# Stores on ScalarE's queue, a pinned order of the first feed-forward products, and the input ahead of the first weight tiles, in a two-block transformer kernel

## The chip, the cores and the metric

The kernel runs on one core of a Trainium2 chip. The metric is the device time of one execution in microseconds, as the median of several runs. The engines are TensorE (PE), VectorE (DVE), ScalarE (ACT), GpSimd (POOL) and SyncE (SP). Every engine takes its own instructions in order. A transfer (DMA) is started by an instruction in the queue of an engine; in the kernel before, all transfers are started by SP.

## What is computed

Two blocks on a sequence of 1024 tokens with 1024 features, all in float32. The part around the main change is the feed-forward of the first block and what stands before it:

```
h = h + concat(o, y) @ w_out
u2 = rmsnorm(h, ln2_g)
a, b = split(u2 @ w_gate_upffn, 2)          # 1024 x 5632
h = h + (silu(a) * b) @ w_down
h = h + sigmoid(rmsnorm(h, ln3_g) @ w_ple_gate) * (p @ w_ple_proj)
```

The first block begins with `rmsnorm(x, ln1_g) @ w_in`; the second one (gated spatial mixing, a convolution and window attention) starts from a layer norm of the first block's result.

## The kernel before, in words

**Split products.** Every float32 operand is split into a hi and a lo part (`Weights.split`, lines 119 to 141, and `split`, lines 343 to 352: ACT copies the hi part, DVE subtracts to get the lo part). `mm3` (line 321) does three matmuls per 128 rows of the contraction: hi x hi (L327), the second operand's lo part (L328), the first operand's lo part (L329). A group of four such k steps is 12 matmuls.

**Order.** The text of the kernel gives each instruction a priority, in the order of the program. A planner (`schedule_with_timeline_sim`, line 1698) runs through the program with its own durations and appends to each engine's queue what is ready, by priority. `keep_in_program_order` ties an instruction behind the one traced before it on its engine. On the chip each queue is then followed strictly.

**The start** (`run`, line 1586): the identity, then `load_x(0)`, which loads four blocks of x (512 KB each) and puts the first tile of `w_in` between the second and the third; then `load_constants`, with `ln1_g`; then two more weight tiles. `norm_in` (line 475) transposes x on PE (L487), splits the columns times `ln1_g` (L350, L351) and saves copies of them (`save_xT`, L519); the squares for the norm are L500. `proj` then does the first products.

**Before the feed-forward** (lines 1615 to 1619): the out projection of the second half of the tokens goes on while `first_operands` makes the operands A11 and A12 from the first half. Then `ple_proj` (line 909, 16 products of six matmuls from `pT`, each copied from PSUM by ACT, L923, and stored to `ppT`, L924) is interleaved with `other_operands` (line 868). That one normalizes the second half (L854) and makes S3 (L885), A22, S1 (L889), S2 (L893) and S4 (L897): for each of four column groups one DVE subtraction or addition in place, then a hi copy on ACT and a lo subtraction on DVE (L347, L348).

**The feed-forward** (`ffn_up`, line 962) works on 22 tiles f of 128 hidden columns with seven products of 12 matmuls each in place of eight (the scheme of Strassen and Winograd). The two token halves give A11, A12, A22, S1 to S4; the two weight tiles give B11, B21, B22 and T1 to T4, made in `up_weights` (line 928) with four POOL subtractions (L946, L947, L948, L951) and four splits. The four PSUM banks of a tile are X = A11 B11 + A12 B21, Z = S3 T3 + A22 T4, V = S1 T1 + S4 B22, Y = S2 T2. Tiles with even f use the PSUM group g, which `ple_proj` uses too, and the weight buffers hi0 to hi2 and lo0 to lo2; odd tiles use group x and three slots `wo`.

**Slots.** Operand tiles of 8 KB per partition are taken from a list of slots, first in, first out. At the end of `other_operands` the list holds, in this order, the slots of a21, a11, a12 (the activations of the two halves, overwritten in place on the way to S1, S2 and S4) and of `stat`. f=0 takes a21's slot for B22; f=1 takes a11's for B11 and B21, a12's for T1 and T3, and `stat`'s for T2 and T4. A tile in a slot can be written when the last reader of the former tile is done. For a11 these are the S2 split of its fourth group (L348) and the fourth L897.

**Buffers.** Six buffers of 128 x 512 (`t512`) rotate among all short-lived tiles, the copies of L923 among them; three raw buffers take weight tiles (L95), and a load waits until the former raw tile has been read. All loads and stores are in SP's queue, so a waiting load holds back the stores behind it. `spill_x2` (line 1168) copies the transposed result of the first block and stores it to `xres` (L1182), 16 times.

Of the kernel before, what the change touches and what calls it, by code (L numbers as in the profile page):

```python
# [22 lines left out]
NF = FFN // 128  # L23
# [145 lines left out]
class Kernel:  # L169
# [148 lines left out]
        return cols[-4:] + cols[-8:-4]  # L318


    def mm3(self, ps, pairs, start=True, stop=True, more=False):


        mm = partial(self.nc.tensor.matmul, skip_group_check=True) if more else self.nc.tensor.matmul
        n = len(pairs)
        for i, ((lh, ll), (rh, rl)) in enumerate(pairs):
            mm(out=ps, lhsT=lh, rhs=rh, start=start and i == 0, stop=False)  # L327
            mm(out=ps, lhsT=lh, rhs=rl, start=False, stop=False)  # L328
            mm(out=ps, lhsT=ll, rhs=rh, start=False, stop=stop and i == n - 1)  # L329

# [100 lines left out]
    def load_vectors(self, names):  # L431

        nc, I = self.nc, self.I
        rows = self.t512()
        ps = self.psx()
        c0 = self.vcol[names[0]]
        r = 0
        for name in names:
            a = I[name]
            n = int(np.prod(a.shape)) // 128  # L440
            flat = a if len(a.shape) == 1 else (a[0] if len(a.shape) == 2 else a[0].rearrange("a b -> (a b)"))
            nc.sync.dma_start(out=rows[r:r + n, 0:128], in_=flat.rearrange("(n p) -> n p", p=128))
            r += n
        nc.tensor.transpose(ps[:, 0:r], rows[0:r, 0:128], self.ident[0:r, 0:r])
        nc.vector.tensor_copy(out=self.vec[:, c0:c0 + r], in_=ps[:, 0:r])
# [15 lines left out]
    def load_x(self, hf):  # L461
        xt, xs = [], []
        for j in range(2):
            t = self.slot([128, 2, D], F32, "x", base=True)
            for i in range(2):
                r0 = hf * NH + (2 * j + i) * 128
                self.nc.sync.dma_start(out=t[:, i, :], in_=self.I["x"][0, r0:r0 + 128, :])
                xt.append(t[:, i, :])
                if hf == 0 and len(xt) == 2:
                    self.wts.load()  # L470
            xs.append(t)
        self.x_tiles[hf] = (xt, xs)
        return xt, xs
# [435 lines left out]
    def ple_proj(self, pt):  # L909

        nc, W = self.nc, self.wts
        yield
        for m in range(8):
            if m % 4 == 0:
                w2 = W.get("w_ple_proj", 0, 2, m * 128, 512)
                if m == 0:
                    W.ahead()
            w = [x[:, :, m % 4 * 128:m % 4 * 128 + 128] for x in w2]
            for hf in range(2):
                ps = self.psg()  # L920
                self.gemm(ps, w, self.pT[hf])
                o = self.t512()
                nc.scalar.activation(out=o, in_=ps, func=ACTF.Copy)  # L923
                nc.sync.dma_start(out=self.ppT[hf, :, m, :], in_=o)  # L924
                yield
        self.release(*pt)

# [34 lines left out]
    def ffn_up(self, A):  # L962

        nc = self.nc
        self.up_slots = self.up_last = None

        def product(ps, a, b, more=False):
            (ah, al), (bh, bl) = A[a], B[b]
            self.mm3(ps, [((bh[:, k, :], bl[:, k, :]), (ah[:, k, :], al[:, k, :])) for k in range(4)], not more,
                     more=more)  # L970

        def copy(ps):
            t = self.t512()
            nc.scalar.activation(out=t, in_=ps, func=ACTF.Copy)  # L974
            return t

        B = self.up_weights(0)
        for f in range(NF):
            tag = "gx"[f % 2]
            X, Z, V, Y = (self.psg(tag) for _ in range(4))  # L980
            product(X, "A11", "B11")
            y1 = copy(X)
            product(Z, "S3", "T3")
            z7 = copy(Z)
            product(X, "A12", "B21", True)
            product(V, "S1", "T1")
            v5 = copy(V)
            nxt = self.up_weights(f + 1) if f + 1 < NF else None
            s1 = self.t512()
            nc.scalar.activation(out=s1, in_=X, func=ACTF.Silu)  # L990
            nc.gpsimd.tensor_tensor(out=v5, in0=v5, in1=z7, op=ALU.add)  # L991
            product(Z, "A22", "T4", True)
            product(Y, "S2", "T2")
            u2 = y1
            nc.vector.tensor_tensor(out=u2, in0=Y, in1=u2, op=ALU.add)
            s2 = z7
            nc.vector.tensor_tensor(out=s2, in0=Z, in1=u2, op=ALU.add)
            nc.scalar.activation(out=s2, in_=s2, func=ACTF.Silu)
            nc.vector.tensor_tensor(out=v5, in0=v5, in1=u2, op=ALU.add)
            product(V, "S4", "B22", True)  # L1000
            nc.vector.tensor_tensor(out=v5, in0=v5, in1=s2, op=ALU.mult)
            nc.sync.dma_start(out=self.sT[f, :, 1, :], in_=v5)
            nc.vector.tensor_tensor(out=u2, in0=V, in1=u2, op=ALU.add)
            nc.vector.tensor_tensor(out=u2, in0=u2, in1=s1, op=ALU.mult)
            nc.sync.dma_start(out=self.sT[f, :, 0, :], in_=u2)
            B = nxt
            if 2 <= f < 10:
                nc.sync.dma_start(out=self.bias_scr[f - 2], in_=self.bias_row[f - 2:f - 1, :].to_broadcast([128, 512]))
        for t in A.values():
            self.release(*t)  # L1010
        self.release(self.up_last, *self.up_slots)
# [156 lines left out]
    def spill_x2(self, hf, N):  # L1168

        nc = self.nc  # L1170
        h = N["h"]
        for t in range(4):
            for k in range(2):
                ps = self.psx()
                for j in range(4):
                    ins = nc.tensor.transpose(ps[:, j * 128:(j + 1) * 128], h[k][:, j, t * 128:(t + 1) * 128], self.ident)
                    if j == 0:
                        self.tc.keep_in_program_order(ins)
                o = self.t512()
                nc.scalar.activation(out=o, in_=ps, func=ACTF.Copy, scale=ALPHA)  # L1180
                r0 = hf * NH + t * 128
                nc.sync.dma_start(out=self.xres[r0:r0 + 128, k * 512:(k + 1) * 512], in_=o)  # L1182
                yield
        self.release(*h)

# [400 lines left out]
    def run(self):  # L1586
        nc = self.nc
        R = [{}, {}]
        N = [{}, {}]
        with self.banks_by(g=4, x=4):  # L1590
            with self.scope():
                self.load_identity()
                self.load_x(0)
                self.load_constants()
                while self.wts.n_raw < Weights.RAW:
                    self.wts.load()
                tiles, act = self.norm_in(0, R[0])
                self.load_vectors(VEC_ROWS[1:])
                self.gla_setup()
                for _ in self.proj(0, act, tiles, R[0]):  # L1600
                    pass
                tiles, act = self.norm_in(1, R[1])
                gla = self.gla_all(R)
                run_both(self.proj(1, act, tiles, R[1]), gla, 29, 68, True)
                self.stat = self.slot([128, 4, NH], F32, "stat", base=True)
                run_both(self.out_proj(0, R[0], N[0]), gla, 9, 30)
            with self.scope(4):
                A = {}
                self.load_taps()
                self.setup2()  # L1610
                steps = self.out_proj(1, R[1], N[1])
                next(steps)
                self.spill_h(0, N[0])
                pt = self.load_pT()
                run_both(steps, self.first_operands(N[0], A), 8, 8)
                self.spill_h(1, N[1])
                run_both(self.ple_proj(pt), self.other_operands(N, A), 18, 15)
                self.release(self.stat)
                self.ffn_up(A)
                self.ffn_down(N)  # L1620
            with self.scope(5):
                self.statz = self.slot([128, 2, NH], F32, "statz", base=True)
                for _ in self.ple(0, N[0]):
                    pass
                run_both(self.ple(1, N[1]), self.norm_mid(0, N[0]), 5, 18)
                self.mix2(N)
# [75 lines left out]
```

## Time and profile before

| | us |
|---|---|
| median of 3 runs | 1683.01 |
| lowest and highest run | 1682.51, 1684.98 |
| the profiled execution, its own time | 1684.41 |
| its span, first to last instruction | 1682.6 |
| PE busy | 1649.3 (98%), 7865 matmuls |
| DVE busy | 1055.2 (63%) |
| ACT busy | 766.0 (46%) |
| POOL busy | 340.5 (20%) |
| mean granted clock of PE, share of full speed | 0.995 |

The time of a run holds the span and some 2 us around it. Busy time counts the instructions that compute; instructions that start a transfer or wait are not in it. The figure in brackets is the share of the span.

### The profile page before, as it was taken

To read this page: it belongs to the slowest core of one execution; us is meant where nothing else is said; L and a number is where in the kernel's file an instruction comes from. 1 tells how busy PE (TensorE), PEld (TensorE's weight loads), DVE (VectorE), ACT (ScalarE), POOL (GpSimd) and SP (SyncE) were. 2 spreads that over 40 slices of the span, in tenths; PEclk is the share of its full clock that TensorE was granted. 3 is DMA by queue.
4 is the path that set the end of the run, shared out by engine and by line. 5 is a ranking of instruction groups with operands and counts; after the bars stand their busy time and mean duration, and the time that the engine had idled before them with its cause. 6 is when DMAs were issued, how large, how long until landed. Compare 5 with 4: busy or idle time off the path is not lost. (4 is left out here: it accounts for less than half of the span.)

```text
span 1682.6 us, 21049 instructions
## 1 busy us (share of the span) xinstructions
PE 1649.3 (98%) x7865; PEld 1375.8 (82%) x7865; DVE 1055.2 (63%) x1608; ACT 766.0 (46%) x1217; POOL 340.5 (20%) x289
## 2 busy tenths in 40 slices
PE   8999999999989999999999999999999999999997
PEld 6888997888867888888888888888878898888786
DVE  4254554777788555565554545236897699737896
ACT  5433357235555333333333433124686632567763
POOL 2011010300026434444340002003000010023453
PEclk9999999999989999999999999999999999999999
DMA  9766434537843222223226962243866622664111
GB/s 313 220 205 200 154 117 121 163 101 225 292 154 110 95 78 85 79 81 95 75 91 220 382 232 88 92 143 98 281 194 226 233 64 63 213 213 175 51 63 63
DMA packets 225631, 258.70 MB, mean 154 GB/s; under 512 B 11063, under 2 KB 175305, under 8 KB 223993
## 3 DMA queue, kind: packets, MB, share of 16 engines
q1 hardware_dynamic: 225528, 257.35, 46.4%
q8 instruction: 62, 1.02, 0.2%
q14 instruction: 41, 0.33, 0.1%
HBM read 186.98 MB, written 72.43 MB: 154 GB/s over the span
## 5 line engine op out<-in xcount | busy, mean ns | idle before, releaser
L327 PE MATMUL g<-ah,wh 128*128 128x512 f32 x896 | 353.6, 398 | 4.6 <-ACT wh L130 2.0
L328 PE MATMUL g<-al,wh 128*128 128x512 f32 x896 | 353.8, 396 | 1.2 <-DVE al L1164 1.2
L329 PE MATMUL g<-ah,wl 128*128 128x512 f32 x896 | 351.2, 393 | 0.0
L130 ACT ACTIVATE wh<-wr 128x1024 fp32r<-128x1024 f32 (+1 forms) x142 | 150.2, 1060 | 271.4 <-PE g L328 155.1
L327 PEld LDWEIGHTS g<-ah,wh 128*128 128x128 f32 x896 | 168.4, 188 | 42.4 <-ACT wh L130 3.9
L328 PEld LDWEIGHTS g<-al,wh 128*128 128x128 f32 x896 | 168.8, 188 | 39.6 <-issue 3.0
L329 PEld LDWEIGHTS g<-ah,wl 128*128 128x128 f32 x896 | 168.6, 188 | 35.1 <-issue 1.8
L135 DVE TENSOR_TENSOR wl<-wr,wh 128x1024 fp32r<-128x1024 f32 (+1 forms) x86 | 108.1, 1258 | 112.1 <-ACT wh L130 105.2
L348 DVE TENSOR_TENSOR s<-sr,s 128x1024 fp32r<-128x1024 f32 x36 | 43.8, 1223 | 61.1 <-ACT s L347 60.7
L1350 DVE SCALAR_TENSOR_TENSOR cacc<-ypad,vec,cacc 128x1024 f32<-128x1024 f32 x60 | 76.7, 1307 | 0.3
L991 POOL TENSOR_TENSOR t<-t,t 128x512 f32<-128x512 f32 x22 | 40.7, 1848 | 178.1 <-ACT t L974 178.1
L809 POOL TENSOR_TENSOR stat<-t,stat 128x512 f32<-128x512 f32 x14 | 23.5, 1704 | 234.5 <-ACT t L808 234.5
L347 ACT ACTIVATE s<-sr 128x1024 fp32r<-128x1024 f32 x36 | 37.8, 1055 | 69.0 <-PE x L329 51.0
L328 PE MATMUL g<-s,wh 128*128 128x512 f32 x176 | 68.5, 389 | 0.0
L329 PE MATMUL g<-s,wl 128*128 128x512 f32 x176 | 68.5, 389 | 0.0
L328 PE MATMUL x<-s,wh 128*128 128x512 f32 x176 | 68.5, 389 | 0.0
L329 PE MATMUL x<-s,wl 128*128 128x512 f32 x176 | 68.5, 389 | 0.0
L327 PE MATMUL g<-s,wh 128*128 128x512 f32 x176 | 67.5, 389 | 0.0
L327 PE MATMUL x<-s,wh 128*128 128x512 f32 x176 | 67.5, 389 | 0.0
L946 POOL TENSOR_TENSOR sr<-wr,wr 128x512 f32<-128x512 f32 x22 | 29.7, 1352 | 158.0 <-DMA wr<-w_gate_upffn 129.7
L328 PE MATMUL g<-S,wh 128*128 128x512 f32 x132 | 51.7, 392 | 3.4 <-DVE S L348 3.4
L327 PE MATMUL g<-wh,ah 128*128 128x256 f32 (+1 forms) x192 | 54.9, 289 | 0.0
(372 smaller groups left out, 3903.2 us busy)
## 6 DMA issues: line engine op xcount, KB each, us to landing
wr<-w_in SPq DMA_DIRECT2D x86, 512.0 KB
low<-wl SPq DMA_DIRECT2D x54, 512.0 KB
wl<-low SPq DMA_DIRECT2D x54, 512.0 KB
wr<-w_gate_upffn SPq DMA_DIRECT2D x44, 512.0 KB
sr<-sT SPq DMA_DIRECT2D x36, 512.0 KB
sT<-t SPq DMA_DIRECT2D x44, 256.0 KB
wr<-w_down SPq DMA_DIRECT2D x22, 512.0 KB
wr<-w_out SPq DMA_DIRECT2D x16, 512.0 KB
```

What stands on the lines that cost most here:

```text
L130: self.nc.scalar.activation(out=hi[:, :n], in_=t[:, :n], func=ACTF.Copy)
L135: self.nc.vector.tensor_tensor(out=lo[:, :n], in0=t[:, :n], in1=hi[:, :n].bitcast(F32), op=ALU.subtract)
L327: mm(out=ps, lhsT=lh, rhs=rh, start=start and i == 0, stop=False)
L328: mm(out=ps, lhsT=lh, rhs=rl, start=False, stop=False)
L329: mm(out=ps, lhsT=ll, rhs=rh, start=False, stop=stop and i == n - 1)
L347: nc.scalar.activation(out=hi, in_=src, func=ACTF.Copy)
L348: (eng or nc.vector).tensor_tensor(out=lo, in0=src, in1=hi.bitcast(F32), op=ALU.subtract)
L809: (eng or nc.gpsimd).tensor_tensor(out=acc, in0=sq, in1=acc, op=ALU.add)
L946: nc.gpsimd.tensor_tensor(out=t13[:, 0, :], in0=b12, in1=b11, op=ALU.subtract)
L991: nc.gpsimd.tensor_tensor(out=v5, in0=v5, in1=z7, op=ALU.add)
L1350: nc.vector.scalar_tensor_tensor(out=acc, in0=src, scalar=w, in1=acc, op0=ALU.mult, op1=ALU.add)
```

## The change

Three transfers move from SP's queue to ACT's: the load of `ln1_g`, the stores to `ppT` and the stores to `xres`. `load_constants` stands before `load_x(0)`, and the first weight tile is loaded after x, with the other two. In `ffn_up` the first two tiles are opened together: the first matmul of A11 B11 of f=0, then of f=1, then of A12 B21 of both, then of S3 T3 of each is tied behind what PE was given before it. f=1's copy of A11 B11 gets a buffer of its own. From f=2 on the order of the program is as before.

```diff
-    def mm3(self, ps, pairs, start=True, stop=True, more=False):
+    def mm3(self, ps, pairs, start=True, stop=True, more=False, pin=False):
...
-            mm(out=ps, lhsT=lh, rhs=rh, start=start and i == 0, stop=False)
+            ins = mm(out=ps, lhsT=lh, rhs=rh, start=start and i == 0, stop=False)
+            if pin and i == 0:
+                self.tc.keep_in_program_order(ins)
...
-            nc.sync.dma_start(out=rows[r:r + n, 0:128], in_=flat.rearrange("(n p) -> n p", p=128))
+            (nc.scalar if c0 == 0 else nc.sync).dma_start(out=rows[r:r + n, 0:128], in_=flat.rearrange("(n p) -> n p", p=128))
...
-                if hf == 0 and len(xt) == 2:
-                    self.wts.load()
...
-                nc.sync.dma_start(out=self.ppT[hf, :, m, :], in_=o)
+                nc.scalar.dma_start(out=self.ppT[hf, :, m, :], in_=o)
...
-        B = self.up_weights(0)
-        for f in range(NF):
+        def begin(f, B, y1=None):
             tag = "gx"[f % 2]
             X, Z, V, Y = (self.psg(tag) for _ in range(4))
-            product(X, "A11", "B11")
-            y1 = copy(X)
-            product(Z, "S3", "T3")
+            product(X, "A11", B["B11"], pin=f < 2)
+            return X, Z, V, Y, copy(X, y1)
+
+        def end(f, B, banks, nxt):
+            X, Z, V, Y, y1 = banks
+            product(Z, "S3", B["T3"], pin=f < 2)
             z7 = copy(Z)
-            product(X, "A12", "B21", True)
-            product(V, "S1", "T1")
+            if f >= 2:
+                product(X, "A12", B["B21"], True)
+            product(V, "S1", B["T1"])
             v5 = copy(V)
-            nxt = self.up_weights(f + 1) if f + 1 < NF else None
+            out = nxt()
...
+        B = [self.up_weights(0)]
+        first = [begin(0, B[0])]
+        B.append(self.up_weights(1))
+        first.append(begin(1, B[1], self.temp([128, 512], "y1")))
+        for f in range(2):
+            product(first[f][0], "A12", B[f]["B21"], True, True)
+        end(0, B[0], first[0], lambda: None)
+        nxt = end(1, B[1], first[1], lambda: self.up_weights(2))
+        for f in range(2, NF):
+            nxt = end(f, nxt, begin(f, nxt), lambda: self.up_weights(f + 1) if f + 1 < NF else None)
...
-                nc.sync.dma_start(out=self.xres[r0:r0 + 128, k * 512:(k + 1) * 512], in_=o)
+                nc.scalar.dma_start(out=self.xres[r0:r0 + 128, k * 512:(k + 1) * 512], in_=o)
...
                 self.load_identity()
+                self.load_constants()
                 self.load_x(0)
-                self.load_constants()
```

## Rows read from the trace of the kernel before

**Rows 1.** Waits of PE over the span: us in total, times, longest us.

```profile
PE g L487 <- DMA x<-x: 6.4, 2, 5.2
PE g L327 <- ACT t L923: 4.9, 3, 3.7
PE g L328 <- DVE S L348: 3.4, 1, 3.4
```

**Rows 2.** Busy us of each engine in stretches, granted clock, DMA share, GB/s.

```profile
465.00:520.00 55.00, 45.71 (x176) 35.36 (x175) 45.28 (x60) 30.53 (x50) 18.08 (x9) 0.91 0.43 147
520.00:905.00 385.00, 385.00 (x1700) 318.79 (x1699) 217.66 (x207) 135.41 (x186) 162.84 (x101) 1.00 0.28 88
1290.00:1345.00 55.00, 54.98 (x272) 44.84 (x271) 35.61 (x40) 37.87 (x53) 3.02 (x2) 1.00 0.74 247
...
480.00:485.00 5.00, 3.34 (x8) 2.67 (x9) 5.00 (x8) 1.46 (x3) 0.00 (x0) 0.54 0.30 114
...
479.09:515.75 36.66, 28.53 (x101) 21.50 (x102) 35.03 (x49) 23.45 (x40) 9.57 (x4) 0.86 0.33 119
```

**Rows 3.** PE in order of time, 467 to 541: start us, us, idle before.

```profile
467.74 0.39 PE L327 MATMUL g<-pT,wh 128*128 128x512 f32 x1
...
477.54 0.39 PE L329 MATMUL g<-pT,wl 128*128 128x512 f32 x1
481.66 0.79 PE L327 MATMUL g<-pT,wh 128*128 128x512 f32 x1 [3.73 <-ACT t L923]
...
496.19 0.50 PE L328 MATMUL g<-S,wh 128*128 128x512 f32 x1 [3.39 <-DVE S L348]
...
506.51 0.40 PE L329 MATMUL g<-pT,wl 128*128 128x512 f32 x1
...
540.64 0.39 PE L327 MATMUL g<-A,wh 128*128 128x512 f32 x1
```

**Rows 4.** Line 924 (ns, min/median/max), then SP, ACT, POOL, DVE in order of time.

```profile
L924 SPq DMA_DIRECT2D ppT<-t x16: 319/320/509, 470.0 to 510.4; - x16
...
475.30 0.38 SPq L95 DMA_DIRECT2D wr<-w_gate_upffn  x1
475.80 34.90 SPq L924 DMA_DIRECT2D ppT<-t  x15
...
481.01 1.08 ACT L923 ACTIVATE t<-g 128x512 f32<-128x512 f32 x2 [4.85 <-DMA ppT<-t]
...
489.21 1.65 POOL L946 TENSOR_TENSOR sr<-wr,wr 128x512 f32<-128x512 f32 x1 [13.94 <-DVE wl L348]
...
512.33 1.05 ACT L347 ACTIVATE wo<-wr 128x1024 fp32r<-128x1024 f32 x1
...
513.44 2.31 DVE L348 TENSOR_TENSOR wo<-wr,wo 128x1024 fp32r<-128x1024 f32 x1
```

**Rows 5.** Groups of DVE, 467.7 to 516: busy us, mean ns, idle before.

```profile
L348 DVE TENSOR_TENSOR S<-h,S 128x512 fp32r<-128x512 f32 x12 | 7.7, 681 | 0.0
L854 DVE SCALAR_TENSOR_TENSOR h<-h,vec,stat 128x512 f32<-128x512 f32 x8 | 5.4, 745 | 0.0
...
L893 DVE TENSOR_TENSOR h<-h,h 128x512 f32<-128x512 f32 x4 | 2.6, 680 | 0.0
```

**Rows 6.** All engines in order of time at the start, 0 to 15.

```profile
9.45 1.22 DVE L135 TENSOR_TENSOR wl<-wr,wh 128x1024 fp32r<-128x1024 f32 x1 [9.45 <-ACT wh L130]
...
9.71 1.06 ACT L500 ACTIVATE E<-x 128x1024 f32<-128x1024 f32 x1 [0.29 <-DMA x<-x]
...
11.06 1.06 ACT L500 ACTIVATE E<-x 128x1024 f32<-128x1024 f32 x1 [0.20 <-DMA x<-x]
...
12.50 2.42 ACT L350 ACTIVATE ah<-g,vec 128x512 fp32r<-128x512 f32 x4 [0.29 <-DVE vec L445]
...
13.89 0.68 DVE L519 COPY t<-g 128x512 f32<-128x512 f32 x1
...
14.72 0.47 PE L327 MATMUL g<-ah,wh 128*128 128x512 f32 x1 [1.17 <-DVE t L519]
```

More of the change, by code (lines that the diff above doesn't have):

```diff
@@ L965, in ffn_up, with product, copy @@
         self.up_slots = self.up_last = None
-        def product(ps, a, b, more=False):
-            (ah, al), (bh, bl) = A[a], B[b]
+        def product(ps, a, b, more=False, pin=False):
+            (ah, al), (bh, bl) = A[a], b
             self.mm3(ps, [((bh[:, k, :], bl[:, k, :]), (ah[:, k, :], al[:, k, :])) for k in range(4)], not more,
-                     more=more)
-        def copy(ps):
-            t = self.t512()
+                     more=more, pin=pin)
+        def copy(ps, t=None):
+            t = t or self.t512()
             nc.scalar.activation(out=t, in_=ps, func=ACTF.Copy)
             return t
-        B = self.up_weights(0)
-        for f in range(NF):
+        def begin(f, B, y1=None):
             tag = "gx"[f % 2]
             X, Z, V, Y = (self.psg(tag) for _ in range(4))
-            product(X, "A11", "B11")
-            y1 = copy(X)
-            product(Z, "S3", "T3")
+            product(X, "A11", B["B11"], pin=f < 2)
[3 more added lines that the diff above has]
+            product(Z, "S3", B["T3"], pin=f < 2)
             z7 = copy(Z)
-            product(X, "A12", "B21", True)
-            product(V, "S1", "T1")
+            if f >= 2:
+                product(X, "A12", B["B21"], True)
+            product(V, "S1", B["T1"])
             v5 = copy(V)
-            nxt = self.up_weights(f + 1) if f + 1 < NF else None
+            out = nxt()
             s1 = self.t512()
@@ L991, in ffn_up @@
             nc.gpsimd.tensor_tensor(out=v5, in0=v5, in1=z7, op=ALU.add)
-            product(Z, "A22", "T4", True)
-            product(Y, "S2", "T2")
+            product(Z, "A22", B["T4"], True)
+            product(Y, "S2", B["T2"])
             u2 = y1
@@ L999, in ffn_up @@
             nc.vector.tensor_tensor(out=v5, in0=v5, in1=u2, op=ALU.add)
-            product(V, "S4", "B22", True)
+            product(V, "S4", B["B22"], True)
             nc.vector.tensor_tensor(out=v5, in0=v5, in1=s2, op=ALU.mult)
@@ L1005, in ffn_up @@
             nc.sync.dma_start(out=self.sT[f, :, 0, :], in_=u2)
-            B = nxt
             if 2 <= f < 10:
                 nc.sync.dma_start(out=self.bias_scr[f - 2], in_=self.bias_row[f - 2:f - 1, :].to_broadcast([128, 512]))
+            return out
+        B = [self.up_weights(0)]
[8 more added lines that the diff above has]
+            nxt = end(f, nxt, begin(f, nxt), lambda: self.up_weights(f + 1) if f + 1 < NF else None)
         for t in A.values():
```

## The prediction, made before the changed kernel was built or run

> **What bounds the kernel now.** I read four views. First the list of waits of TensorE (PE), the engine that does the products and is hardly ever idle: only its idle time and its slow time can be won. The longest waits are 6.4 us for x at the start, 4.9 us for copies of line 923 and 3.4 us for an S operand [rows 1]. Second, busy time by stage: of 465 to 520 PE works 45.71 of 55 us; from 520 to 905 it works all the time, 385 us for 1700 products, so 0.2265 us a product [rows 2]. Whatever is won at 480 is thus kept until 905. Between 1290 and 1345, where the other moved stores lie, PE works 54.98 of 55 us: nothing can be won there. Third, PE in order of time at the feed-forward entry [rows 3]: the first p product at 467.74; the queue stands still after 477.54 until a copy at 481.01 frees a bank; it waits again for S operands until 496.19. In between the granted clock falls, 0.54 in 480 to 485 [rows 2]; that is near the lower of its two levels (1.2 of 2.4 GHz). The products of tile f=2 begin at 540.64. From 467.74 to there the program has 96 p products, 2 column sums and 2 x 84 products: 266 x 0.2265 = 60.3 us. It took 72.9. **The entry loses 12.6 us**: 9.3 idle, 3.3 by the clock. Fourth, the other queues there [rows 4]: SP's load at 475.30 waits for a raw buffer, the stores behind it go out from 475.80, and ACT can write its next copy only at 481.01, when a store has landed. DVE is busy 35.03 us of the 36.66 from 479.09 to 515.75 [rows 2]: the operands come at DVE's pace.
>
> **The stores of line 924 on ACT's queue.** A store now goes out right behind its copy, whatever SP waits for. Without the stall the 98 products that start at 467.74 end 22.2 us later, at 489.9, where before the last p product begins at 506.51 [rows 3]. Price: an issue takes 0.32 us on SP (319 to 509 ns) [rows 4]; ACT has never issued one here, so I bound it by 0 and 0.51 and take 0.32, the median for the same transfer. 16 x 0.32 = 5.1 us on ACT, which works 30.5 of the 55 us [rows 2]; a copy and an issue (0.6 + 0.32) fit into the 1.36 us of six products. So nothing is lost on the path. If ACT had no room, the copies would hold the banks again. Six buffers rotate, 8.2 us long; a store that takes 5.2 us (475.80 to 481.01) does not hold them.
>
> **The pins.** After the p products PE may take A11·B11 of f=0 (12 products, until 492.6), then must take A11·B11 of f=1, A12·B21 of both and only then S3·T3 of f=0. A22·T4 of f=0 adds into S3·T3's bank and waits too. What is late next is the weight half of f=1. Its hi and lo parts go into a slot that the first-half activations a11 hold until the last S4 subtraction and the last S2 split have read them. The trace shows it: the raw tile is there at 489.21, since POOL works on it, yet ACT splits it only at 512.33 and DVE ends the lo part at 515.75 [rows 4], though ACT idled 4.9 us before 481.01. The change does not move that slot. So **the gate is the operand chain of DVE**, the same as before: it starts at 479.09, needs 35.0 us of work and loses only the 1.6 us gap; the half is complete at 514.1. Until then PE can do the 98, A11·B11 of f=0, and what is not pinned: S1·T1, S2·T2, S4·B22 of f=0, 146 products or 33.1 us. Loss until then 514.1 - 467.74 - 33.1 = 13.3 us, against 12.6: +0.7 us. Then 48 products and more are ready, and the queue does not stop before f=2.
>
> The lo part at 513.44 took 2.31 us with POOL at work beside it; the same operation took 1.22 us at 9.45 with POOL idle [rows 4, 6]. With 1.22 the gate opens at 513.0 and the entry comes to -0.4 us. POOL's work for f=1 can move ahead of it, since its buffers come free with the p products. I take 0.0, between the two. The Trainium skill (SBUF — State Buffer, "SBUF: two separate sides") says that GpSimd and a VectorE operation with two SBUF inputs take a shared port pair in turn, each for a whole instruction; the 2.31 us agree, and by that rule the sum would be +0.7 where POOL still runs there and -0.4 where not.
>
> **The start.** Before, w_in's first tile is loaded between x's second and third block. The squares show the landings: the third block at 9.71, the fourth at 11.06 [rows 6]. Without the weight tile in front the fourth lands where the third did, 1.35 us earlier; ln1_g comes through ACT's empty queue, which ends the 0.29 us wait of the first operand at 12.50. So the operand starts at about 10.9, and the bank that its product needs is free 2.1 us later, as before (12.50 to 14.57): the first product at 13.0, not 14.72, a gain of 1.7 us. Against it, the split of the first weight tile (ACT 1.06, DVE 1.22 us) lay in a wait before and now lies among the operands: if all of DVE's 1.22 us is on the path the gain is 0.5 us. I take 1.2; ends 0.5 and 1.7. The DMA engines carry the same bytes in both, so the third tile lands as before.
>
> **The stores of line 1182 on ACT's queue.** 16 issues, 5.1 us on ACT, which works 37.87 of those 55 us [rows 2]; PE waits for nothing there. I take 0, bounds 0 and +1 if a copy holds a bank.
>
> **Sum:** 0.0 - 1.2 + 0 = -1.2 us on the profiled execution (1684.4 us with 1682.6 of span, 1.4 above the median). On the median of 1683.0: **1681.8 us**. The runs shown span 2.5 us; 0.2%, 3.4 us, is about what a measurement of this kernel can tell from no change.
>
> **Rivals.** (A) The chain is reordered, so that a11 comes free earlier. DVE must at least do line 854's 5.4 us, four rows of 2.6 us like line 893's and four S2 splits of 0.68 [rows 5]: 479.09 + 5.4 + 10.4 + 2.7 = 497.6; with the splits (1.05 and 1.22) the half is there at 499.9. PE has done 110 products by then: it loses 7.3 us, and up to 3.3 more by the clock, which is what both falls cost before; I take 2.4. 9.7 against 12.6: -2.9, with the start -4.1, 1678.9 us. For it: lines 854 to 897 don't need ACT and can run ahead. Against it: before, DVE did splits and subtractions in turn, and the planner follows program order. (B) Slower: a wait at the pins in place of the one removed. The half is complete at 515.75 as before, and PE has only 134 products to do until then (S4·B22 is queued behind the pinned ones): it loses 48.0 - 30.4 = 17.6, and 2.4 by the clock as in A: 20.0 against 12.6, +7.4, with the start +6.2, 1689.2 us. It decides once the half comes later than the S2 operands and S4·B22 can't fill. For it: the order of DVE's last instructions. (C) The slot doesn't hold, because the half gets another free one: PE goes on from 489.9 with 48 ready products, S3 is there by 500.8, and only the S4 operands (514.1 against PE's 511.7 at the earliest) cost some 3 us. -9.6, with the start 1672.2 us. Against it: ACT's late split at 512.33. That the stores don't help at all is part of B: the gate is the same.
>
> **Numbers.** Forecast 0.47: the gate follows from the code and shows in the trace, the sum lies within 1 us. A 0.17, C 0.13, B 0.23. Faster by over 0.2% is A and C, 0.30; slower is B, 0.23; the rest within. The range leaves out C's middle and what lies above B's: 1675.0 to 1689.2. The forecast's own range, from its bounds (entry -2 to +3, start -1.7 to -0.5, +1), is 1679 to 1686.
>
> **What would show it.** No wait of PE for line 923 and none of ACT for a store; p products ended by about 490; the first product with f=1's half (x<-A,wo) at 511 to 514 behind a wait of PE for a wo split, in place of S; f=2 beginning at 540 to 541. At the start the first L327 product at 13.0 to 14.2. Wrong if x<-A,wo starts before 505 (A, C), or if f=2 begins after 545 (B).

## The result and the profile after

| | before | after |
|---|---|---|
| median of six runs each, us | 1682.90 (1682.26 to 1684.98) | 1692.88 (1691.81 to 1693.97) |
| profiled execution, its span | 1684.4, 1682.6 | 1693.97, 1692.0 |
| last store to sT begins (end of the feed-forward's first half) | 927.09 | 936.88 |

The changed kernel is slower: ratio 1.0059, 95% interval 1.0049 to 1.0070, 10.0 us of medians against a forecast of -1.2 us and a range that ended at 1689.2. Nearly all of it, 9.8 us, is there when the last sT store goes out.

Waits of PE in the changed kernel (us in total, times, longest us):

```profile
PE g L327 <- ACT t L923: 8.2, 4, 6.1
PE g L327 <- ACT wh L130: 6.3, 2, 4.7
PE x L327 <- ACT wo L349: 3.8, 1, 3.8
```

Against [rows 1]: the wait for line 923, which the moved stores were to remove, has grown from 4.9 to 8.2 us. Two others are new: the 4.7 us for ACT's split of a weight tile at the start (line 130; the kernel before waits 0.3 us for such a split there, and both wait 1.6 us for one later on), and the wait for ACT's split of a weight half at the feed-forward entry (wo). Busy time in stretches; the columns are the stretch, its length, then busy us (and instructions) of PE, PE's weight load, DVE, ACT and POOL, then the granted clock, the DMA share and GB/s. First the changed kernel, then 15 to 20 us of the kernel before:

```profile
15.00:20.00 5.00, 3.15 (x6) 1.55 (x7) 5.00 (x8) 5.00 (x8) 0.00 (x0) 0.50 1.03 409
...
0.00:20.00 20.00, 10.05 (x39) 8.15 (x40) 8.71 (x15) 14.98 (x23) 3.66 (x15) 0.87 0.95 319
...
465.00:520.00 55.00, 42.41 (x166) 31.62 (x164) 42.89 (x60) 29.30 (x49) 33.95 (x8) 0.94 0.43 150
520.00:560.00 40.00, 39.22 (x161) 32.23 (x162) 22.60 (x22) 16.44 (x22) 19.43 (x13) 0.92 0.34 103
1290.00:1345.00 55.00, 55.00 (x270) 44.88 (x269) 33.32 (x42) 36.95 (x52) 3.08 (x2) 1.00 0.66 222
```

```profile
15.00:20.00 5.00, 4.68 (x20) 3.21 (x19) 5.00 (x9) 5.00 (x8) 0.00 (x0) 1.00 0.92 349
```

Before, PE did 20 products between 15 and 20 us at full clock. After, the same stretch has six at half of it (0.50). So there are two places of loss, the start and the entry; 1290 to 1345, where the moved xres stores lie, is as full as before (55.00 of 55, [rows 2]).

**The start**, changed kernel, ACT, PE and DVE in order of time (start us, us; in brackets the idle time before and its releaser):

```profile
10.91 2.42 ACT L352 ACTIVATE ah<-g,vec 128x512 fp32r<-128x512 f32 x4 [0.56 <-PE g L487]
13.20 2.44 ACT L352 ACTIVATE ah<-x,vec 128x512 fp32r<-128x512 f32 x4
15.48 2.05 ACT L130 ACTIVATE wh<-wr 128x1024 fp32r<-128x1024 f32 x2
...
16.64 0.80 PE L327 MATMUL g<-ah,wh 128*128 128x512 f32 x1 [4.70 <-ACT wh L130]
...
18.70 3.48 DVE L135 TENSOR_TENSOR wl<-wr,wh 128x1024 fp32r<-128x1024 f32 x3
```

The operands come earlier, as forecast: the first ah copy begins at 10.91, not 12.50 [rows 6]. But the weight tile is now split behind all eight ah copies, on ACT at 15.48 and on DVE at 18.70, where before its low part was begun at 9.45 [rows 6]. The first product waits 4.70 us for it, starts at 16.64 and takes 0.80 us, where the first one before took 0.47 [rows 6]: the 0.50 granted here is the lower of the clock's two levels (1.2 of 2.4 GHz).

**The entry**, changed kernel, in order of time:

```profile
496.93 1.20 ACT L923 ACTIVATE t<-g 128x512 f32<-128x512 f32 x2 [0.57 <-DVE S L350]
...
497.58 0.80 PE L327 MATMUL g<-pT,wh 128*128 128x512 f32 x1 [6.06 <-ACT t L923]
...
506.68 0.40 PE L331 MATMUL g<-pT,wl 128*128 128x512 f32 x1
...
516.35 0.39 PE L327 MATMUL x<-A,wo 128*128 128x512 f32 x1
516.58 0.39 PE L330 MATMUL x<-A,wo 128*128 128x512 f32 x1
...
519.67 2.00 ACT L349 ACTIVATE wo<-sr 128x1024 fp32r<-128x1024 f32 x2 [5.64 <-POOL sr L951]
...
520.78 0.79 PE L327 MATMUL x<-S,wo 128*128 128x512 f32 x1 [3.81 <-ACT wo L349]
...
553.16 0.39 PE L327 MATMUL g<-A,wh 128*128 128x512 f32 x1
```

Read from below: f=2 begins at 553.16. Before, it began at 540.64 [rows 3] with 12 products of f=1 still to do (2.7 us at 0.2265), so the loss up to here is 9.8 us, and the sT stores carry it on. Part of it was brought along from the start. The last product of the out projection, first before, then after:

```profile
467.52 0.39 PE L329 MATMUL g<-ah,wl 128*128 128x512 f32 x1
```

```profile
472.37 0.39 PE L331 MATMUL g<-ah,wl 128*128 128x512 f32 x1
```

The changed kernel has done five p products (1.1 us) by then, the kernel before none: PE comes 3.7 us late, and the entry itself loses 6.1. At 520.78 PE waits for x<-S,wo: that is S2 T2 of f=1, whose T2 is made from POOL's differences (sr). The product stands third behind x<-A,wo, the opened tile f=1, and with it stands everything behind it in PE's queue. POOL and DVE at that time:

```profile
491.56 23.28 POOL L946 TENSOR_TENSOR sr<-wr,wr 128x512 f32<-128x512 f32 x1 [14.57 <-DVE wl L350]
514.81 2.27 POOL L947 TENSOR_TENSOR sr<-wr 128x512 f32<-128x512 f32 x1
...
518.38 1.26 POOL L951 TENSOR_TENSOR sr<-wr,sr 128x512 f32<-128x512 f32 x1
...
495.62 1.89 DVE L350 TENSOR_TENSOR S<-t,S 128x512 fp32r<-128x512 f32 x3
...
513.01 0.68 DVE L350 TENSOR_TENSOR S<-h,S 128x512 fp32r<-128x512 f32 x1
514.07 1.86 DVE L350 TENSOR_TENSOR wo<-wr,wo 128x1024 fp32r<-128x1024 f32 x1 [0.38 <-ACT wo L349]
```

The first difference for f=1 took 23.28 us; before, the same instruction took 1.65 [rows 4]. It ended at 514.84, 0.8 us after the end of DVE's first pause (0.38 us, until 514.07). All that DVE does from 491.40 until that pause has two inputs in SBUF. The Trainium skill (SBUF — State Buffer, "SBUF: two separate sides") says that such an operation and one of GpSimd lock each other out of a shared pair of ports for a whole instruction each; the trace agrees, and goes beyond it: POOL did not get a turn in between. In the kernel before, POOL's later differences for f=1 were late as well:

```profile
509.45 5.22 POOL L948 TENSOR_TENSOR sr<-wr,sr 128x512 f32<-128x512 f32 x1 [16.88 <-DVE wl L348]
514.75 2.15 POOL L951 TENSOR_TENSOR sr<-wr,sr 128x512 f32<-128x512 f32 x1
...
527.04 0.39 PE L327 MATMUL x<-S,wo 128*128 128x512 f32 x1
```

The third one (L948) first waited for a buffer that DVE freed with its split of f=0's pair (wl), and then took 5.22 us. They ended at 516.90, and nothing waited, since the old order reached x<-S,wo only at 527.04. So a late operand became a stall by the new order, not by being later.

### The profile page after: what moved, and what is told of

The parts are those of the page before. It is cut to its first block, busy times and chain, and to the rows that moved or that the text cites. A ratio compares the mean times of both kernels' runs of the same rounds, so it can differ in the third digit from the quotient of the medians.

```text
span 1692.0 us, 21028 instructions
## 1 busy us (share of the span) xinstructions
PE 1653.0 (98%) x7865; PEld 1377.8 (81%) x7865; DVE 1050.5 (62%) x1608; ACT 766.9 (45%) x1217; POOL 353.3 (21%) x289
## 5 line engine op out<-in xcount | busy, mean ns | idle before, releaser
L946 POOL TENSOR_TENSOR sr<-wr,wr 128x512 f32<-128x512 f32 x22 | 51.0, 2319 | 161.6 <-DMA wr<-w_gate_upffn 136.4
L327 PE MATMUL x<-S,wo 128*128 128x512 f32 x132 | 51.8, 392 | 3.8 <-ACT wo L349 3.8
```

The lines of the kernel that those rows point to most:

```text
L327: ins = mm(out=ps, lhsT=lh, rhs=rh, start=start and i == 0, stop=False)
L946: nc.gpsimd.tensor_tensor(out=t13[:, 0, :], in0=b12, in1=b11, op=ALU.subtract)
```

## The experiments

All times below are medians; the kernel before measured 1682.5 to 1682.9 us in these runs. Where a stage is read from one execution it is that execution's; the same kernel's executions differ by up to 5 us, so verdicts rest on the ratios.

**1. Which part costs: halves of the change.** The first kernel is the changed one with the old start:

```diff
-                self.load_constants()
                 self.load_x(0)
+                self.load_constants()
...
+                if hf == 0 and len(xt) == 2:
+                    self.wts.load()
```

(ln1_g also goes back to SP's queue.)

> The changed kernel with the start of the kernel before (first weight tile between x's blocks, constants after x, ln1_g through SP). Theory 1: the change loses twice, at the start some 4.9 us (the last out-projection product ends 4.9 us later than before) and at the feed-forward entry some 4.5. Then this run is 4 to 5.5 us above the kernel before, about 1687.7. Rival: the start only shifts the work and the whole loss is made at the entry: then it stays 9 to 10 us above, about 1692.5.

Measured: 1688.76 us, ratio 1.0031 (1.0020 to 1.0043): 6.0 us, a little above the 4 to 5.5 expected.

The second is the kernel before with the new start alone, the same lines the other way round.

> The kernel before with the new start alone. Theory 1: 4 to 5.5 us above the kernel before (about 1687.8), with a first product of w_in at about 16.6 us, since ACT splits the first weight tile behind all eight operand copies. Rival (the start is innocent): within 1 us of the kernel before.

Measured: 1685.63 us, 1.0015 (1.0006 to 1.0023): 2.9 us, between the theory and the rival. Its first product:

```profile
16.22 0.80 PE L327 MATMUL g<-ah,wh 128*128 128x512 f32 x1 [5.19 <-ACT wh L130]
```

The third is the kernel before with the ppT stores on ACT's queue alone:

```diff
-                nc.sync.dma_start(out=self.ppT[hf, :, m, :], in_=o)
+                nc.scalar.dma_start(out=self.ppT[hf, :, m, :], in_=o)
```

> The kernel before with the ppT stores on ACT's queue alone. Theory 1: the copies no longer wait for a store but then for a rotating buffer that holds an S3 difference until DVE has split it, so the time is within 2 us of the kernel before, and the wait of PE for a copy is still there, some microseconds later. Rival (the stores are the gain and the pins throw it away): the copy stall of 6 us, idle and clock, goes, about 1677.

Measured: 1681.42 us, 0.9995 (0.9986 to 1.0004). PE's longest waits from 455 to 560:

```profile
PE g L328 <- DVE S L348: 4.6, 1, 4.6
PE g L327 <- ACT t L923: 2.1, 3, 1.0
```

The time is as expected; of the wait for the copies less is left than expected. In the old order it falls from 4.9 to 2.1 us [rows 1], and the wait for the S operand grows from 3.4 to 4.6.

The fourth is the kernel before with the new order of `ffn_up` alone: begin, end and the pins as in the change, all stores on SP's queue, the old start.

> The kernel before with the pinned opening of tiles f=0 and f=1 alone (stores and start as before). Theory 1: PE waits for the f=1 weight half or for f=1's T2 and T4, which POOL delivers late, 3 to 6 us above the kernel before. Rival (the pins cost nothing, the stores' new place does): within 1.5 us of the kernel before.

Measured: 1688.72 us, 1.0036 (1.0022 to 1.0050). Its profiled execution was the shortest of five, 1685.48 us:

```profile
486.03 1.65 POOL L948 TENSOR_TENSOR sr<-wr,wr 128x512 f32<-128x512 f32 x1 [13.26 <-DVE wl L350]
...
514.87 0.50 PE L327 MATMUL x<-S,wo 128*128 128x512 f32 x1 [1.25 <-ACT wo L349]
```

The same product stops PE here, for 1.25 us instead of 3.8, with POOL's first difference (L948 in this kernel's lines) at 1.65 us. What the other four did is not shown.

What follows: the pinned order costs 6.0 us by itself, and with both store moves added it is the same (1688.76): the stores neither help nor hurt beside it. The new start costs 2.9 us alone and 4.1 in the changed kernel (1692.88 - 1688.76); the two differ by less than their intervals. 6.0 + 4.1 makes the 10.

**2. The copy stall.** In the kernel of the first experiment the copy of line 923 is held up as in the changed one. The four S3 differences get a slot of their own instead of t512, the six rotating buffers that the copies use too:

```diff
+        diff = self.slot([128, 4, NH], F32, "diff")
         yield from step("S3", s3)
+        self.release(diff)
...
-            t = self.t512()
+            t = diff[:, k, :]
```

> The changed kernel with the old start (measured 1688.76 us, its 5.71 us wait of PE on the ACT copy L925), and the four S3 differences no longer take the rotating t512 buffers but a slot of their own. Theory (the copy stall is a buffer coupling: the copy waits for a t512 buffer that an S3 difference holds until DVE has split it): the 5.7 us wait falls below 1 us, the p products end 4 to 6 us earlier (about 497 instead of 502.5). Whether the time follows is the second question. Rival 1 (the entry is then gated by f=1's POOL differences and DVE's splits, which this edit leaves): the wait on wo grows from 3.8 to 6 us or more and the time stays within 1687 to 1690. Rival 2 (the copy stall itself is the loss): 1683 to 1685. My own guess 1687.5.

Measured: 1688.20 us, 1.0032 (1.0019 to 1.0044). PE's longest waits from 455 to 560:

```profile
PE g L327 <- ACT S L349: 6.5, 2, 4.9
PE x L327 <- ACT wo L349: 6.4, 1, 6.4
```

No wait for the copy is left, and the last p product begins at 492.31 instead of 502.50, 10.2 us earlier where 4 to 6 were expected: the coupling is shown. The time does not move: PE comes to the next operands earlier and waits there, 6.5 us for S and 6.4 us for the same wo instead of 3.8. Rival 1 holds.

**3. The product in front.** The kernel of the first experiment, with S1 T1 and S2 T2 of f=1 pinned as well:

```diff
-            product(V, "S1", B["T1"])
+            product(V, "S1", B["T1"], pin=f == 1)
...
-            product(Y, "S2", B["T2"])
+            product(Y, "S2", B["T2"], pin=f == 1)
```

PE's order differs in two products alone: the pair x<-S,wo leaves its place as third and fourth after the opening of f=1.

> The changed kernel with the old start (1688.76 us); f=1's first S1*T1 and S2*T2 products are pinned too, so that they stay behind the A12*B21 products that are ready: in the PE order only two products, x<-S,wo, move behind 11 products x<-A,wo. Theory (a product that waits for POOL's late differences stands in PE's in-order queue ahead of ready work): the 3.8 us wait of L327 on ACT wo falls to about 1.3 us (11 products of 0.23 us go into it), the clock falls less, last store of sT 2.5 to 4 us earlier, 1685 to 1686.5 us. Rival (the end of f=1 waits for wo's split whatever stands in front of it, since DVE's split at about 519 comes last): the wait only moves behind, 1688 to 1689 us.

Measured: 1683.52 us, 1.0002 (0.9993 to 1.0011). The products x<-A,wo named there are the rest of A11 B11; A12 B21 comes later. PE's longest wait from 455 to 560:

```profile
PE g L327 <- ACT t L925: 9.2, 5, 6.4
```

The wait for wo is gone, not shortened to 1.3, and 5.2 us come back: more than the 3.8 of the wait, since the clock does not fall behind it (0.94 granted from 465 to 520 and 1.00 from 520 to 560, against 0.89 and 0.98). POOL's first difference for f=1 took 23.29 us here too: with the pair out of the way its lateness costs nothing. The copy stall stands as long as ever and costs nothing that can be measured against the kernel before.

**4. Why that operand is late.** The kernel of the first experiment, f=1's four differences on DVE instead of POOL:

```diff
-        nc.gpsimd.tensor_tensor(out=t13[:, 0, :], in0=b12, in1=b11, op=ALU.subtract)
+        (nc.vector if f == 1 else nc.gpsimd).tensor_tensor(out=t13[:, 0, :], in0=b12, in1=b11, op=ALU.subtract)
```

(and the other three likewise)

> The changed kernel with the old start (1688.76 us); the four weight differences of f=1 are made on DVE instead of POOL (about 0.7 us each, 2.8 us in all between its splits). Theory (POOL gets no turn while DVE runs back to back, its first subtraction took 23.29 us instead of 1.65, and f=1's T2 and T4 are late by this alone): the differences stand before 507 us, ACT splits wo<-sr by 511 instead of 515.5, PE's wait for wo falls below 1.5 us, last sT store 3 to 5 us earlier, 1684 to 1686 us. Rival (DVE is the bound of the entry, its 2.8 us more go on the path): wo later or the S splits later, 1688 to 1691 us.

Measured: 1684.60 us, 1.0010 (1.0002 to 1.0019). DVE and ACT:

```profile
492.80 0.68 DVE L948 TENSOR_TENSOR sr<-wr,wr 128x512 f32<-128x512 f32 x1
...
508.99 0.68 DVE L953 TENSOR_TENSOR sr<-wr,sr 128x512 f32<-128x512 f32 x1
...
510.63 1.05 ACT L349 ACTIVATE wo<-sr 128x1024 fp32r<-128x1024 f32 x1
```

The inputs of the first were there by 492.80, and each difference takes 0.68 us. PE waits for no wo; 4.2 us come back though DVE has 2.8 more to do. The last difference stands at 509.7, not at 507 as expected, since the third still has to wait for f=0's buffer (it begins at 507.18). On POOL, in the kernel of the first experiment, the last stood at 515.5. So 5.8 us of the lateness were made by POOL's instructions, not by their inputs. The planner also moved a few products and copies in the queues of PE and ACT, so this edit is less clean than that of 3. That the ports held them up rests on the rows and the page; no run took the ports away.

**5. The order at the start.** The kernel of the second run, ACT's split of the first weight tile pinned in front of the eight ah copies; the DMAs keep their order:

```diff
-        self.nc.scalar.activation(out=hi[:, :n], in_=t[:, :n], func=ACTF.Copy)
+        ins = self.nc.scalar.activation(out=hi[:, :n], in_=t[:, :n], func=ACTF.Copy)
+        if i == 0:
+            self.tc.keep_in_program_order(ins)
```

(and the ah copies of the first half likewise)

> The kernel before with the new start (1685.63 us, first product 16.22 us, PE waiting 5.19 us for wh), ACT's split of the first weight tile pinned ahead of its eight ah copies; DMA order as in the new start. Theory (the order on ACT and DVE costs, not the landing): the first weight tile has landed by about 10.7 us, ACT copies it then, the first product begins at 12.3 to 13.5 us, the PE wait for wh falls below 3 us, last sT store about 925 to 927 us, time 1681 to 1683.5. Rival (the first weight tile lands too late behind the four blocks of x): ACT waits for wr until 12 us or later, all ah copies come later by as much, first product after 14.5 us and 1684.5 to 1687 us.

Measured: 1683.22 us, 1.0006 (0.9997 to 1.0015).

```profile
11.29 1.06 ACT L131 ACTIVATE wh<-wr 128x1024 fp32r<-128x1024 f32 x1 [0.60 <-DMA wr<-w_in]
12.37 2.42 ACT L353 ACTIVATE ah<-g,vec 128x512 fp32r<-128x512 f32 x4
...
15.00 0.76 PE L330 MATMUL g<-ah,wh 128*128 128x512 f32 x1 [3.95 <-DVE t L522]
```

Each theory is right by half. The tile lands 0.6 us late for ACT, and the first product, at 15.00, misses the 13.5 of the theory; it now waits for the bank. But 2.4 of the 2.9 us come back, so most of the loss was the order. The new start then loses nothing that can be measured, and gains nothing.

The other part of the new start alone, constants in front and ln1_g on ACT's queue, the weight tile where it was:

```diff
+                self.load_constants()
                 self.load_x(0)
-                self.load_constants()
```

> The kernel before with the constants ahead of x and ln1_g through ACT's queue, but the first weight tile still between x's second and third block, so that ACT's order stays as it was. Theory (moving the weight tile is what costs at the start): first operand at 12.2 us, first product 14.3 to 14.8 us, clock of 0 to 20 us 0.98 or more, 1682 to 1683.3 us. Rival (the constants in front delay the first transposes, and the clock falls by that): first product after 15.5 us or the clock below 0.95, 1684 us or more.

Measured: 1681.66 us, 0.9997 (0.9988 to 1.0006). Its first product, then its clock:

```profile
14.33 0.47 PE L327 MATMUL g<-ah,wh 128*128 128x512 f32 x1 [2.34 <-DVE t L519]
```

```profile
15.00:20.00 5.00, 5.00 (x17) 3.93 (x16) 5.00 (x9) 5.00 (x8) 0.00 (x0) 0.66 1.02 377
```

The time stays, so moving the weight tile is what costs. The rival's sign is there too: the first product is 0.4 us earlier, but PE's pause in front of it is 2.34 us instead of 1.17 [rows 6], since PE's transposes end at 11.99 instead of 13.55 and the small product of the constants (at 11.99 before) no longer stands among them. The clock falls afterwards, 17 products instead of 20 from 15 to 20 us.

**6. Do the two losses add?** The whole changed kernel with the edits of 3 and 5.

> The whole changed kernel (1692.88 us) with both repairs: f=1's first S1*T1 and S2*T2 pinned behind the A12*B21 products (alone -5.2 us), and ACT's split of the first weight tile pinned ahead of the ah copies (alone -2.4 us). Theory (these two orders are the two losses, and they add): 1684.5 to 1686.5 us, last sT store about 929 us. Rival (one loss covers the other, for PE that comes later to the entry waits less there): 1687 to 1690 us. If there is a third loss that neither repair touches: above 1690.

Measured: 1684.76 us, 1.0014 (1.0005 to 1.0023). 8.1 of the 10 us come back, 5.2 + 2.4 = 7.6 were expected: they add. Of what is left, 0.14% or 1.8 us, the start shows a part: the granted clock over the first 20 us is still 0.86, and in this execution PE comes 0.9 us late to the p products (469.51 with five of them done, against 467.52). The rest is not explained.

**7. What bounds the entry without these stalls.** The old start, with the edits of 2, 3 and 4 together.

> The changed kernel with the old start, f=1's products pinned, f=1's differences on DVE and S3's differences in their own slot: each of the three waits found at the entry is taken away at once. Theory (DVE's chain is then what sets the entry, 2.8 us longer): no copy wait over 1 us, no wait for wo over 1 us, a wait for an S operand of 4 to 8 us in their place, 1681 to 1684.5 us. Rival (the waits were the loss and nothing takes their place): below 1679 us.

Measured: 1682.01 us, 0.9994 (0.9986 to 1.0003). PE's waits from 455 to 560:

```profile
PE g L327 <- ACT S L349: 6.5, 2, 4.0
PE g L327 <- ACT t L978: 0.7, 1, 0.7
PE g L330 <- DVE S L350: 0.6, 1, 0.6
PE x L327 <- ACT wo L349: 0.4, 1, 0.4
```

And the kernel before with the edit of 2 and the ppT stores on ACT's queue.

> The kernel before with two edits: the ppT stores on ACT's queue (alone 1681.42 us against 1682.8) and the four S3 differences in a slot of their own instead of t512. Theory (the copy stall is the t512 coupling, and DVE's chain of operands then sets the end of the entry in the old order, so the stall turns into a wait for S): PE's waits for line 923 fall below 1 us, the wait for S grows to 6 us or more, time 1680 to 1682.5 us. Rival (in the old order the removed stall is kept): 1675 to 1679 us. My own guess 1681.

Measured: 1680.84 us, 0.9988 (0.9979 to 0.9997).

```profile
PE x L327 <- ACT wo L347: 6.5, 1, 6.5
PE g L327 <- ACT S L347: 0.9, 1, 0.9
```

In both the copy stall turns into a wait of the same size further on, for S in the first as expected, for wo in the second, where S was expected. There the planner has put x<-S,wo at 512.85 instead of 527.04, and one of POOL's later differences took 8.80 us: the product of experiment 3 again, in front without a pin. The second is the only kernel here whose interval lies below 1, by 2 us, less than the 0.2% that the forecast took for measurable.

## Why the prediction was wrong

**What held.** That what is won or lost at the entry is kept held: 9.8 us at the last sT store, 10.0 at the end. That the xres stores cost nothing held (PE 55.00 of 55 us; 0.326 us for an issue on ACT, against 0.32 taken).

**Failed: "the queue does not stop before f=2".** The prediction counted 48 products as ready once f=1's half was there, and they were. It did not ask what PE had been given third. A queue that is followed in order stops at its first product that isn't ready, however many are behind it; here that was S2 T2 of f=1, with the latest of all operands. Experiment 3 moves this pair alone and gives 5.2 of the entry's 6.0 us back. Tile f=2 began at 553.16, beyond the 545 that the forecast had named as a sign of being wrong.

**Failed beside it: POOL's work "can move ahead".** The forecast weighed POOL only as a brake on one DVE split (2.31 against 1.22 us) and gave POOL's own work no price; its one row of it is of 1.65 us [rows 4]. The other direction, DVE holding up POOL, was not priced: 23.28 us. The rows at 509.45 and 514.75 of the kernel before would have shown T2 and T4 complete no earlier than 516.9. The long hold does not come from the pins: the kernel before with the new start alone has it too (23.29 us) and waits for no wo. It makes the stop longer; the order makes it.

**Failed: without the stall the 98 products were to end "at 489.9".** The last of them began at 506.68 (with the old start at 502.50), and the stall grew to 6.06 us. "Six buffers rotate" took the stores for their only holders. The S3 differences take from the same six and hold them until DVE has split them; in the kernel before a store happened to be the last to let go, in the changed one it was DVE. The Trainium skill (Trainium Kernel Development and Optimization, "Key Constraints") says that issuing DMAs from several engines saves only issue time; the third run's time agrees, 0.9995, though PE waited 2.8 us less for the copies. This step was wrong in its mechanism but cost nothing, as experiments 2 and 3 show.

**The loss before was summed too low.** The forecast's 12.6 us take 266 products for done when f=2 begins at 540.64. Twelve of f=1 were still to come, so 254 were done, 57.5 us of work in 72.9: the old entry lost 15.4 us, 9.3 idle and 6.1 at the lower clock and in smaller gaps. With that the forecast's own steps would have given -2.1 us for the entry instead of +0.7, further from what came.

**The gate was not where it was put.** f=1's half in a11's slot was to be complete at 514.1. With the old start it was there at 511.8 (DVE's split of wo at 509.89 takes 1.87 us), and PE came to it without a wait. So rival B, which had the right sign and an entry loss of 7.4 us against 6.0 measured, did not have the mechanism: the wait came behind the pins, not at them.

**The start: the sign was wrong.** The first operand (10.9 forecast, 10.91 measured) and its bank (free at 13.0 by both) were right. The step that failed is that the split of the first weight tile "now lies among the operands", priced at up to DVE's 1.22 us. It lay behind them all: 4.6 us of ah copies on ACT in front (10.91 to 15.48), a wait of 4.70 us, and products at the lower clock after it. That price was bounded by the duration of the moved instruction; the bound should have been the length of the work that it can be placed behind.

**The range** reached to 1689.2 by B with a gain at the start. B's entry with the start as measured, +7.4 + 4.1, would have made 1694.5: with the start's sign right the range would have held 1692.88, but by luck, since B's mechanism is not what happened.

## What to carry to other kernels

Moving work forward moves its operands' deadlines too: before an order is pinned, list for each product right behind the pin which engine makes its operand and when that ended in the trace, and keep those that come late behind work that is ready. A step that loses its place in a wait can end up behind everything the planner finds ready, so bound its cost by that work and not by its own length. And a wait taken away at one place of a chain that another engine paces (here DVE's operands and POOL's differences) shows up again at the next place, so look there before counting it as won.

## What the runs showed of the hardware

- A two-input subtraction on POOL, 128x512, took 23.28 us beside DVE working without a pause on operations with two SBUF inputs, and 1.26 to 2.27 us elsewhere in the same stretch; it ended 0.8 us after DVE's first pause, of 0.38 us. On DVE the same subtraction took 0.68 us. With the ppT stores on ACT's queue alone it took 17.92 us and ended 0.75 us after a DVE pause of 0.39 us; with the new start alone it took 23.29 us, and no pause of DVE is seen before its end, only a DVE split stretched to 2.32 us:

```profile
487.26 17.92 POOL L946 TENSOR_TENSOR sr<-wr,wr 128x512 f32<-128x512 f32 x1 [14.57 <-DVE wl L348]
...
504.43 1.83 DVE L348 TENSOR_TENSOR wl<-sr,wh 128x1024 fp32r<-128x1024 f32 x1 [0.39 <-ACT wh L347]
```

```profile
491.17 23.29 POOL L944 TENSOR_TENSOR sr<-wr,wr 128x512 f32<-128x512 f32 x1 [13.18 <-DVE wl L348]
```

Why the same instruction got through in 1.65 us in the kernel before, with DVE busy beside it at 1.36 us a split (4.07 us for three) instead of 0.63, stays open:

```profile
489.05 4.07 DVE L348 TENSOR_TENSOR A<-h,A 128x512 fp32r<-128x512 f32 x3
```

- After a pause of PE of 2.34 us behind transposes, three products ran at the higher level of the clock and the next ones at the lower (0.63 us each from 15.47 to 18.03; 0.66 granted from 15 to 20 us); after one of 1.17 us the clock stayed (1.00). No run changes the pause alone.
